# Attention's value products: three single-pass matmuls on split operands against plain float32 in two column halves, with a written order on TensorE

## The chip, the cores and the metric

The kernel runs on one core of one Trainium2 chip. The metric is the device time of one execution in microseconds (us); the number given for a kernel is the median of several runs. TensorE (PE in the profile, PEld for its weight loads) multiplies matrices into PSUM banks, VectorE (DVE), ScalarE (ACT) and GpSimd (POOL) do the element-wise work, SyncE (SP) issues the DMAs.

## What is computed

Two layers over 1024 latent tokens and 256 context tokens of width 1024, all in float32. Each layer normalises and modulates its input, projects it to queries, keys, values and a gate, attends, and projects back. Layer 0 is grouped-query attention (16 heads of 64, 4 key/value heads) for latent and context tokens; layer 1 is latent attention (16 heads, queries and keys of 96, values of 64) for latent tokens alone. Latent queries read all 1280 keys, context queries the 256 context keys. The part that the change touches:

```python
def gqa_attend(q, k, v):
    s = jnp.einsum('bqhgd,bkhd->bhgqk', q, k).astype(jnp.float32) * (GQA_HEAD_DIM ** -0.5)
    p = jax.nn.softmax(s, axis=-1).astype(v.dtype)
    return jnp.einsum('bhgqk,bkhd->bqhgd', p, v)
...
    y = (o * jax.nn.silu(g)) @ p["w_out"]
```

## The kernel before

**Precision.** Most products are made of three matmuls: each operand is split in a high part (rounded to the one-pass type float32r) and a low part (the rest), and high x high, high x low and low x high add up in PSUM (`mm3`, lines 85 to 87; the split, lines 78 and 79). A few small products, such as the modulation ones of line 211, are given to TensorE in plain float32; the profile shows each of those as two matmul instructions, and their operands lie on strips of 32 output partitions, four strips to a bank.

**Stages.** Modulation vectors, keys and values of layer 0, queries, gates, attention of layer 0, its output projection (which also prepares layer 1), then keys and values, queries, gates, attention and output projection of layer 1. What a stage hands to a later one goes through DRAM. Values go there as two arrays, `vdh` and `vdl`, with columns of the constant 2 and 0 beside each head's 64 columns (`v_stages`), so that a value matmul of 128 columns gives a head's outputs and its softmax sums (doubled) at once; the gate is stored doubled as well.

**Attention** (`class Attention`). A unit of work is one head with its 1024 queries and ten key tiles of 128 (`lat`), or, in layer 0, the four heads of a key group with the context queries and two key tiles (`ctx`): 16 + 4 units in layer 0, 16 in layer 1. For each unit:

- Ten *maxima* (`do_max`, lines 364 to 372): two matmuls of 512 columns (or four of 256) fill the scratch tile `mx`, of which there is one, and a DVE reduction takes the maximum of each query row. `do_shift` turns the result with a matmul against the identity (L383) and a DMA puts it as an extra row into the query operand, so that the score matmul subtracts it. Maxima are made ahead: `lead` steps before the scores need them.
- For each key tile, *scores* (`do_scores`): four matmuls in layer 0, six in layer 1, into one of two tiles `st` (L421); two exponentials of it on ACT, `ph` in float32r and `p32` in float32 (L424, L426); their difference `pl` on DVE (L428).
- For each key tile, *values* (`do_av`, L442): six matmuls, three products for each half of 512 queries.
- At its end `finish`: the outputs are copied from PSUM (L465), the sums go by DMA into 128 rows, are inverted on DVE (L489), go to a DRAM row, come back spread over 64 partitions (L494); GpSimd multiplies by the gate and by the outputs (L502, L503), and a DMA stores them. These steps are deferred by one to five key tiles (`later`).

`run` goes through the key tiles: scores, whatever is deferred, a maximum, then the values of the key tile before. The order on TensorE there is chosen by the scheduler that builds the program; elsewhere a block `with in_order(engine)` keeps the written order. The output projection (`out_proj`) starts on the first seven pairs of heads and takes the eighth when the last units are stored.

Of the kernel before, what the change touches and what calls it, by code (L numbers as in the profile page):

```python
# [10 lines left out]
F32 = mybir.dt.float32  # L11
# [8 lines left out]
P = 128  # L20
# [15 lines left out]
def hybrid_kernel(ctx: ExitStack, tc: tile.TileContext, ins: dict, out: bass.AP):  # L36
# [15 lines left out]
    pool.memset(mhalf, -0.5)  # L52

# [14 lines left out]
    vdh = [dram.tile([4, TT, P, w], F32, name=f"vdh{w}") for w in (192, 384)]  # L68
    vdl = [dram.tile([4, TT, P, w], F32, name=f"vdl{w}") for w in (192, 384)]
# [246 lines left out]
    class Attention:  # L316
        def __init__(self, l, units, ops):
# [9 lines left out]
            self.todo = []  # L327

# [7 lines left out]
        def open_late(self, st, stp):  # L336
            l = self.l
            self.op = st.enter_context(tc.tile_pool(name=f"op{l}", bufs=2, reuse_waits="tile"))
            self.vp = stp.enter_context(tc.tile_pool(name=f"vp{l}", bufs=self.ops["vbufs"], reuse_waits="tile"))
            self.pp = stp.enter_context(tc.tile_pool(name=f"pp{l}", bufs=3, reuse_waits="tile"))  # L340
# [4 lines left out]
        def load_v(self, u):  # L345
            key = (u["vg"], u["vc"])
            if key not in self.vcache:
                vs = {}
                for kt in u["kts"]:
                    a = self.vp.tile([P, self.ops["vw"]], F32R, name="vh", tag="vh")  # L350
                    b = self.vp.tile([P, self.ops["vw"]], F32R, name="vl", tag="vl")
                    sp.dma_start(raw(a), vdh[self.l][u["vg"], kt][:, u["vc"]:u["vc"] + 192])
                    sp.dma_start(raw(b), vdl[self.l][u["vg"], kt][:, u["vc"]:u["vc"] + 192])
                    vs[kt] = (a, b)
                self.vcache = {key: vs}
            return self.vcache[key]
# [17 lines left out]
        def do_shift(self, u):  # L374
# [6 lines left out]
            def turn():  # L381
                t = self.ps_m.tile([P, 1024], F32, name="mx", tag="mx")
# [5 lines left out]
            self.later((1, turn))  # L388
# [26 lines left out]
        def do_scores(self, u, kt):  # L415
# [7 lines left out]
            ph = self.pp.tile([P, 1024], F32R, name="ph", tag="ph")  # L423
            act.activation(ph, ps, AF.Exp, scale=self.ops["scale"])  # L424
            p32 = self.pp.tile([P, 1024], F32, name="p32", tag="p32", bufs=2)
            act.activation(p32, ps, AF.Exp, scale=self.ops["scale"])  # L426
            pl = self.pp.tile([P, 1024], F32R, name="pl", tag="pl")
            dve.tensor_sub(pl, p32, raw(ph))  # L428
            return ph, pl

        def do_av(self, u, kt, ph, pl):
            s = self.state[id(u)]
            first, last = kt == u["kts"][0], kt == u["kts"][-1]
            if first:
# [9 lines left out]
            if last:  # L444
                self.finish(u)
# [848 lines left out]
```

## Time and profile before

| | us |
|---|---|
| median of 3 runs | 1961.7 (1961.02 to 1970.17) |
| the profiled execution, device time | 1965.52 |
| its span, first to last instruction | 1963.7 |
| TensorE busy | 1887.5 (96%) |
| VectorE busy | 1321.9 (67%) |
| ScalarE busy | 932.1 (47%) |
| GpSimd busy | 557.1 (28%) |

The granted TensorE clock has a mean of 0.987 of full speed. A matmul's row has the start and a modelled duration that overlaps with the next one's; what a stream of matmuls costs is read from the distance of the starts. "Idle before, releaser" names what ended an engine's idle time.

### The profile page before, as it was taken

The page shows a single profiled execution, that of the slowest core. Times are in us where ns is not written, and L with a number is a line of the kernel's source. Part 1 is how long each engine was busy: PE and PEld are TensorE (multiplying, and loading weights), DVE is VectorE, ACT ScalarE, POOL GpSimd, SP SyncE. Part 2 cuts the span into 40 slices and gives each one's busy share as a digit, 9 for nine tenths or more (in the row PEclk, how much of TensorE's full clock was granted, in tenths as well). Part 3 has the DMA queues.
Part 4 walks back from the last instruction along what each step waited for, and adds up shares of the span by engine and source line. Part 5 has one row for each costly group of instructions (what it writes and reads, how often), then busy time and mean ns, then how long its engine had stood idle before and what let it go on. Part 6 is the DMA issues. An engine that isn't in the chain of part 4 may idle for free. (4 is left out here: it accounts for less than half of the span.)

```text
span 1963.7 us, 24408 instructions
## 1 busy us (share of the span) xinstructions
PE 1887.5 (96%) x8728; PEld 1502.7 (77%) x8728; DVE 1321.9 (67%) x1722; ACT 932.1 (47%) x1254; POOL 557.1 (28%) x438
## 2 busy tenths in 40 slices
PE   7889999999999999998989999999999999999999
PEld 2676668777777777776878788977888888888777
DVE  3764541378898899873566766746777787777632
ACT  2421221066676667772234533325666666666610
POOL 2553431022312222123235544423121212121221
PEclk9999999999999999999999999999999999999999
DMA  7676753342422423115445886675434343433152
GB/s 269 223 248 195 238 166 113 95 141 60 108 77 77 119 58 96 49 37 156 129 128 172 284 250 176 181 210 177 120 98 115 105 122 96 115 103 85 27 177 92
DMA packets 249265, 269.54 MB, mean 137 GB/s; under 512 B 34872, under 2 KB 197416, under 8 KB 249144
## 3 DMA queue, kind: packets, MB, share of 16 engines
q1 hardware_dynamic: 249144, 267.98, 46.4%
q8 instruction: 70, 1.15, 0.2%
q14 instruction: 51, 0.42, 0.1%
HBM read 176.94 MB, written 90.67 MB: 136 GB/s over the span
## 5 line engine op out<-in xcount | busy, mean ns | idle before, releaser
L428 DVE TENSOR_TENSOR pl<-p,ph 128x1024 fp32r<-128x1024 f32 x328 | 442.3, 1349 | 93.8 <-ACT p L426 90.3
L424 ACT ACTIVATE ph<-st 128x1024 fp32r<-128x1024 f32 x328 | 337.3, 1028 | 330.9 <-PE st L421 330.9
L366 DVE TENSOR_REDUCE mA<-mx 128x1 f32<-128x1024 f32 x256 | 312.6, 1221 | 109.8 <-PE mx L364 107.5
L426 ACT ACTIVATE p<-st 128x1024 f32<-128x1024 f32 x328 | 334.7, 1020 | 0.0
L502 POOL TENSOR_TENSOR rb<-rb,sg 64x1024 f32<-64x1024 f32 x32 | 81.7, 2554 | 607.1 <-DMA rb<-rrow 577.0
L442 PE MATMUL av<-pl,vh 128*128 128x512 f32 x656 | 214.7, 401 | 10.9 <-DVE pl L428 10.4
L442 PE MATMUL av<-ph,vh 128*128 128x512 f32 x656 | 216.1, 400 | 1.1 <-ACT ph L424 0.9
L442 PE MATMUL av<-ph,vl 128*128 128x512 f32 x656 | 215.1, 392 | 0.0
L442 PEld LDWEIGHTS av<-pl,vh 128*128 128x128 f32 x656 | 120.1, 188 | 52.3 <-DVE pl L428 28.3
L128 POOL TENSOR_TENSOR wb<-wraw,wa 128x512 fp32r<-128x512 f32 (+3 forms) x69 | 91.7, 1349 | 202.6 <-ACT wa L147 202.5
L442 PEld LDWEIGHTS av<-ph,vl 128*128 128x128 f32 x656 | 123.3, 188 | 28.4
L442 PEld LDWEIGHTS av<-ph,vh 128*128 128x128 f32 x656 | 117.2, 189 | 29.1 <-ACT ph L424 2.1
L85 PE MATMUL mm<-wa,hh 128*128 128x512 f32 (+2 forms) x320 | 122.9, 384 | 5.3 <-ACT hh L285 2.5
L87 PE MATMUL mm<-wa,hl 128*128 128x512 f32 (+2 forms) x320 | 119.2, 374 | 0.5 <-DVE hl L128 0.5
L86 PE MATMUL mm<-wb,hh 128*128 128x512 f32 (+2 forms) x320 | 118.7, 371 | 0.0
L85 PE MATMUL y<-wa,oh 128*128 128x512 f32 x288 | 115.9, 402 | 2.6 <-ACT oh L568 2.5
L87 PE MATMUL y<-wa,ol 128*128 128x512 f32 x288 | 114.7, 400 | 2.2 <-DVE ol L569 2.2
L86 PE MATMUL y<-wb,oh 128*128 128x512 f32 x288 | 114.8, 399 | 0.0
L421 PE MATMUL st<-QA,KA 128*128 128x512 f32 x336 | 107.3, 394 | 0.0
L421 PE MATMUL st<-QB,KB 65*128 65x512 f32 x336 | 106.6, 396 | 0.0
L503 POOL TENSOR_TENSOR os<-os,rb 64x1024 f32<-64x1024 f32 x32 | 102.7, 3208 | 2.5
L372 DVE TENSOR_REDUCE mB<-mx 128x4 f32<-128x1024 f32 x72 | 87.9, 1221 | 21.9 <-PE mx L370 21.8
(211 smaller groups left out, 3625.1 us busy)
## 6 DMA issues: line engine op xcount, KB each, us to landing
mraw<-in_l_w_mod SPq DMA_DIRECT2D x96, 256.0 KB
wraw<-in_l_w_in SPq DMA_DIRECT2D x28, 512.0 KB
vh<-vdh SPq DMA_DIRECT2D x122, 96.0 KB
vl<-vdl SPq DMA_DIRECT2D x122, 96.0 KB
vdh<-vsth SPq DMA_DIRECT2D x30, 384.0 KB
vdl<-vstl SPq DMA_DIRECT2D x30, 384.0 KB
xt<-in_x SPq DMA_DIRECT2D x16, 512.0 KB
wraw<-in_l_w_out SPq DMA_DIRECT2D x16, 512.0 KB
```

The costliest lines, as they stand in the source:

```text
L85: pe.matmul(ps, lhsT=lh(k), rhs=rh(k), start=first and i == 0, stop=False)
L86: pe.matmul(ps, lhsT=lh(k), rhs=rl(k), start=False, stop=False)
L87: pe.matmul(ps, lhsT=ll(k), rhs=rh(k), start=False, stop=last and i == len(ks) - 1)
L128: eng.tensor_sub(lo, a, b)
L366: dve.reduce_max(s["mA"][:, i:i + 1], m, axis=AX.X)
L372: dve.reduce_max(s["mB"][:, 4 * i:4 * i + 4], m.rearrange("p (a b) -> p a b", a=4), axis=AX.X)
L421: pe.matmul(ps[:, n * 512:(n + 1) * 512], lhsT=lh, rhs=rf(n), start=(j == 0), stop=(j == len(prods) - 1))
L424: act.activation(ph, ps, AF.Exp, scale=self.ops["scale"])
L426: act.activation(p32, ps, AF.Exp, scale=self.ops["scale"])
L428: dve.tensor_sub(pl, p32, raw(ph))
L442: pe.matmul(s["av"][n], lhsT=v[:, c0:c0 + P], rhs=src[:, n * 512:(n + 1) * 512], start=first and f, stop=last and e)
L503: pool.tensor_mul(o[sl, :], o[sl, :], rb[sl, :])
```

## The change

- **Value products.** Values are stored once, in float32, without constant columns (`vd`), and loaded as one tile for all heads (layer 0) or for two heads (layer 1). `do_av` multiplies p and v in plain float32: one matmul of 64 columns for the first 512 queries into partitions 0 to 63 of a bank, one for the other 512 into partitions 64 to 127.
- **Exponential.** One, in float32; no difference.
- **Sums.** `add_up` adds the p tiles of a unit: tiles 1, 3 and 5 on DVE (two additions, each in two halves of 512 columns), tiles 0, 2, 4, 6, 7, 8, 9 and the DVE sum on GpSimd (seven additions). The last unit of a layer is shared otherwise. `total_up` then sums over partitions with four matmuls against a tile of twos, on four strips of 32 partitions, in the unit's own PSUM tile, and copies the result on ACT.
- **Order.** `run` goes through pairs of key tiles, with TensorE in written order: a maximum, what is deferred, the values of the last but one pair, a maximum, the scores of this pair. What a unit's end defers comes 4 to 12 key tiles later (`lag`). The turned maxima go into the PSUM tile of the unit that ended last (`spare`), two steps later instead of one. `lead` is 14 instead of 12 and 13.
- **Unit's end.** Outputs lie as 128 x 512, so GpSimd's two products are 128 x 512; four DMAs read the sums, two each move gate, inverse and output.

```diff
         def load_v(self, u):
-            key = (u["vg"], u["vc"])
+
+            key, w = u["vg"], self.ops["vw"]
             if key not in self.vcache:
...
+                v = self.vp.tile([P, TT, w], F32, name="v", tag="v")
+                c0 = key[1]
+                sp.dma_start(v, vd[self.l][key[0]].rearrange("t p n -> p t n")[:, :, c0:c0 + w])
+                self.vcache[key] = v
...
             def turn():
-                t = self.ps_m.tile([P, 1024], F32, name="mx", tag="mx")
+                t = self.spare
+                if t is None:
+                    t = self.ps_m.tile([P, 1024], F32, name="mx", tag="mx")
                 pe.transpose(t[:8, :P], c, ident)
...
-            self.later((1, turn))
+            self.later((2, turn))
...
-            ph = self.pp.tile([P, 1024], F32R, name="ph", tag="ph")
-            act.activation(ph, ps, AF.Exp, scale=self.ops["scale"])
-            p32 = self.pp.tile([P, 1024], F32, name="p32", tag="p32", bufs=2)
-            act.activation(p32, ps, AF.Exp, scale=self.ops["scale"])
-            pl = self.pp.tile([P, 1024], F32R, name="pl", tag="pl")
-            dve.tensor_sub(pl, p32, raw(ph))
-            return ph, pl
-
-        def do_av(self, u, kt, ph, pl):
+            p = self.pp.tile([P, 1024], F32, name="p", tag="p")
+            act.activation(p, ps, AF.Exp, scale=self.ops["scale"])
+            self.add_up(u, kt, p)
+            return p
+
+        def add_up(self, u, kt, p):
...
+            by_dve = i % 2 == 1 or i > 5 if tail else i in (1, 3, 5)
+
+            def add(who, p):
+                if who not in sums:
+                    sums[who] = (p, False)
+                    return
+                a, own = sums[who]
+                t = a if own else self.ap.tile([P, 1024], F32, name="ac" + who, tag="ac" + who)
+                if who == "p":
+                    pool.tensor_add(t, a, p)
+                else:
+                    for n in range(2):
+                        ns = slice(n * 512, n * 512 + 512)
+                        dve.tensor_add(t[:, ns], a[:, ns], p[:, ns])
+                sums[who] = (t, True)
+
+            add("d" if by_dve else "p", p)
+            if last:
+                a, b = ("d", "p") if tail or len(u["kts"]) == 2 else ("p", "d")
+                add(a, sums[b][0])
+                s["total"] = sums[a][0]
+
+        def do_av(self, u, group):
...
+            for kt, p in group:
+                for n in range(2):
+                    pe.matmul(s["av"][64 * n:64 * n + 64, :], lhsT=s["v"][:, kt, u["vc"]:u["vc"] + 64],
+                              rhs=p[:, n * 512:(n + 1) * 512], start=kt == kts[0], stop=kt == kts[-1])
...
+            def total_up():
+                t = s["av"]
+                for q in range(4):
+                    pe.matmul(t[32 * q:32 * q + 32, :256], lhsT=twos, rhs=s["total"][:, q * 256:q * 256 + 256],
+                              start=True, stop=True)
+                act.copy(rb[:, :256], t[:, :256])
+                for q in range(4):
+                    sp.dma_start(cs[32 * q:32 * q + 32, :], rb[32 * q:32 * q + 1, :256])
...
-            self.later((1, invert), (2, spread), (3, scale), (5, store))
...
+            self.later((self.lag, total_up), (self.lag + 2, invert), (self.lag + 4, spread), (self.lag + 6, scale),
+                       (self.lag + 8, store))
+
+        lag = 4
...
+            pairs = [(t, u, u["kts"][i:i + 2]) for t, u in enumerate(self.units) for i in range(0, len(u["kts"]), 2)]
+            with in_order(mybir.EngineType.PE):
+                for t, u, kts in pairs:
...
+                    self.maxima(self.step - base + 1 + lead, t + 1 + ahead)
                     self.run_deferred(self.step)
...
+                    if len(held) == 2:
+                        self.do_av(*held.pop(0))
+                    self.maxima(self.step - base + 2 + lead, t + 1 + ahead)
+                    held.append((u, [(kt, self.do_scores(u, kt)) for kt in kts]))
```

TensorE in layer 0's loop before, one key tile and the start of the next (names are output, then moving and stationary operand, each with its buffer's number):

```order
L421 MATMUL st_4002<-QA_3635,KA_2948 128x512 x2
L421 MATMUL st_4002<-QB_3636,KB_2949 128x512 x2
L364 MATMUL mx_4014<-KA_2948,QA_3905 128x512 x2
L442 MATMUL av_3994<-ph_3981,vh_3407 128x512
L442 MATMUL av_3995<-ph_3981,vh_3407 128x512
L442 MATMUL av_3994<-ph_3981,vl_3408 128x512
L442 MATMUL av_3995<-ph_3981,vl_3408 128x512
L442 MATMUL av_3994<-pl_3985,vh_3407 128x512
L442 MATMUL av_3995<-pl_3985,vh_3407 128x512
L421 MATMUL st_4024<-QA_3635,KA_2948 128x512 x2
```

The same place in the loop of the change, one pair of key tiles (lines from 50 on have moved: L423 is the score matmul, L471 the value matmul):

```order
L364 MATMUL mx_4066<-KA_3976,QA_3982 128x512 x2
L471 MATMUL av_4072<-p_4016,v_3402 64x512 x2
L471 MATMUL av_4072<-p_4023,v_3402 64x512 x2
L364 MATMUL mx_4077<-KA_3976,QA_3982 128x512 x2
L423 MATMUL st_4081<-QA_3689,KA_2934 128x512 x2
L423 MATMUL st_4081<-QB_3690,KB_2935 128x512 x2
L423 MATMUL st_4089<-QA_3689,KA_2934 128x512 x2
L423 MATMUL st_4089<-QB_3690,KB_2935 128x512 x2
```

Twelve value matmuls for two key tiles have become four, and they stand between two maxima, with the scores behind them. Once a unit, its end stands there as well; TensorE in layer 0's loop of the change, at the pair where a unit's total (L515) and the turned maxima (L385) are due:

```order
L370 MATMUL mx_3903<-KA_2934,QA_3894 128x256 x4
L515 MATMUL av_3653<-acp_3629,twos_76 32x256 x4
L385 MATMUL av_3653<-ident_69,mC_3875 8x128
L471 MATMUL av_3864<-p_3842,v_3402 64x512 x2
L471 MATMUL av_3864<-p_3851,v_3402 64x512 x2
L370 MATMUL mx_3926<-KA_2934,QA_3894 128x256 x4
```

L385 writes into av_3653, the bank that L515 has just filled and that ACT copies in between; both stand ahead of the values. In the program of the change this is so in 12 pairs of layer 0 and 14 of layer 1. VectorE in the loop of the change, from a unit's last maxima on (L366 and L372 reduce maxima, L453 adds p, L387 makes the extra query row, L523 inverts sums):

```order
L372 TENSOR_REDUCE mB_3495<-mx_3647 128x4
L453 TENSOR_TENSOR acd_3638<-p_3594,p_3636 128x512 x2
L372 TENSOR_REDUCE mB_3495<-mx_3658 128x4
L379 TENSOR_TENSOR mC_3664<-mA_3494,mB_3495 128x8
L366 TENSOR_REDUCE mA_3694<-mx_3696 128x1
L453 TENSOR_TENSOR acd_3638<-acd_3638,p_3679 128x512 x2
L387 TENSOR_SCALAR crow_3710<-av_3459 8x128
L366 TENSOR_REDUCE mA_3694<-mx_3717 128x1
L523 RECIPROCAL cr_3747<-cs_3617 128x8
```

Before, a subtraction (L428) followed each reduction; now a unit's two additions stand between the two reductions of its third and its fourth pair.

178 lines of the change are left out of this document (64 added, 114 removed).

## Prediction

> **What bounds the kernel now.** I read the busy times first, then the two attention stages as windows, then one key tile in the timeline. Part 1 of the page:
>
> ```profile
> PE 1887.5 (96%) x8728; PEld 1502.7 (77%) x8728; DVE 1321.9 (67%) x1722; ACT 932.1 (47%) x1254; POOL 557.1 (28%) x438
> ```
>
> TensorE (PE) is the only engine near full; GpSimd (POOL) has most room. The windows view of the two stages, each from its first score matmul to its last value matmul (columns: length, then busy time and count of PE, weight loads, DVE, ACT, POOL, then clock, DMA share, GB/s):
>
> ```profile
> 403.10:889.80 486.70, 477.31 (x2086) 371.18 (x2085) 423.13 (x376) 344.99 (x380) 110.83 (x45) 1.00 0.30 82
> 1349.50:1868.60 519.10, 516.49 (x2281) 419.04 (x2281) 396.90 (x363) 320.70 (x341) 110.53 (x50) 1.00 0.38 104
> ```
>
> Together 1005.8 us, over half of the span, at full clock; the change works here. One key tile of layer 0, PE's timeline (start, duration, instruction):
>
> ```profile
> 614.07 0.63 PE L421 MATMUL st<-QA,KA 128*128 128x512 f32 x2
> 614.53 0.62 PE L364 MATMUL mx<-KA,QA 128*128 128x512 f32 x2
> 615.00 0.64 PE L421 MATMUL st<-QB,KB 65*128 65x512 f32 x2
> 615.47 0.63 PE L442 MATMUL av<-ph,vh 128*128 128x512 f32 x2
> ...
> 616.40 0.62 PE L442 MATMUL av<-pl,vh 128*128 128x512 f32 x2
> 616.87 0.62 PE L421 MATMUL st<-QA,KA 128*128 128x512 f32 x2
> ```
>
> Durations overlap, so starts count: from 614.07 to 616.87 twelve matmuls issue in 2.80 us, 0.233 us each, without a gap. Four are scores, two a maximum, six the values. So PE's matmul count sets these stages. Groups of the page, and the longest wait of PE's weight loads there:
>
> ```profile
> L442 PE MATMUL av<-ph,vh 128*128 128x512 f32 x656 | 216.1, 400 | 1.1 <-ACT ph L424 0.9
> ```
> ```profile
> PEld av L442 <- DVE pl L428: 28.3, 46, 1.6
> ```
>
> 656/2 = 328 key tiles, 168 in layer 0 and 160 in layer 1. At 0.233 us a matmul, layer 0 would take 168 x 10 x 0.233 + 156 maxima x 0.467 = 465 us, and 487 are measured: 22 us are waits, mostly for the split of p (L428). Layer 1 (six score matmuls, about 146 maxima in the loop): 160 x 12 x 0.233 + 68 = 516 of 519 us.
>
> **The change part by part.**
>
> *Value products.* Six single-pass matmuls a key tile go (1.40 us); two plain float32 matmuls of 64 columns come, on separate column halves. The trace has no 64-column one, but the modulation matmuls (L211) are plain float32, 32 columns wide, on four column strips. One alone (two passes), then four on four strips, between single-pass neighbours:
>
> ```profile
> 29.39 0.40 PE L85 MATMUL mm<-wa,hh 128*128 128x512 f32 x1
> 29.72 1.04 PE L211 MATMUL pm<-mraw,s 128*32 128x512 f32 x2
> 30.70 0.50 PE L85 MATMUL mm<-wa,hh 128*128 128x512 f32 x1
> 31.03 0.62 PE L86 MATMUL mm<-wb,hh 128*128 128x512 f32 x2
> ```
> ```profile
> 261.40 0.39 PE L87 MATMUL mm<-wa,hlc 128*128 128x512 f32 x1
> 261.72 1.06 PE L211 MATMUL pm<-mraw,s 128*32 128x512 f32 x8
> 262.72 0.50 PE L85 MATMUL mm<-wa,hhc 128*128 128x512 f32 x1
> 263.05 0.39 PE L86 MATMUL mm<-wb,hhc 128*128 128x512 f32 x1
> ```
>
> From neighbour to second neighbour 1.64 us and 1.65 us; less the two neighbours' own 0.47 that is 1.17 and 1.18. Four strips cost what one costs: they run side by side. For two rounds on the same strips, the weight loads:
>
> ```profile
> 48.10 0.16 PEld L211 LDWEIGHTS pm<-mraw,s 128*32 128x32 f32 x8 [0.36 <-DMA w_k<-in_l_k_norm]
> ...
> 48.99 0.12 PEld L211 LDWEIGHTS pm<-mraw,s 128*32 128x32 f32 x2 [0.31 <-issue]
> ```
>
> The second pass pair starts 0.89 us after the first, so a round more costs 0.87 or so, and the new step, two key tiles at a time, 1.18 + 0.87 = 2.05 us against 2.80. Of 164 pairs each saves 0.75: **-123 us** (84 pairs in layer 0: -63; 80 in layer 1: -60). The ends for the second half of the columns: free, as these rows say, or behind the first with two passes more, 0.86 us a key tile. I take free, four strips being a harder case than two.
>
> Each strip needs two weight loads a round, and the row at 48.10 has all eight begun and ended within 0.16 us, though one takes 0.11 us by itself (a load of 128 columns 0.19):
>
> ```profile
> L211 PEld LDWEIGHTS pm<-mraw,s x192: 106/109/155, 4.3 to 269.0; 128*32 128x32 f32 x192
> ```
> ```profile
> L442 PEld LDWEIGHTS av<-pl,vh 128*128 128x128 f32 x656 | 120.1, 188 | 52.3 <-DVE pl L428 28.3
> ```
>
> So they lie beside each other and beside matmuls, and cost the sum nothing. [...]
>
> *Maxima, in written order.* The scratch bank mx has one buffer, so a maximum waits for the DVE reduction before it:
>
> ```profile
> 621.56 1.22 DVE L366 TENSOR_REDUCE mA<-mx 128x1 f32<-128x1024 f32 x1
> ...
> 622.90 0.67 PE L364 MATMUL mx<-KA,QA 128*128 128x512 f32 x2
> ```
> ```profile
> 1381.84 0.63 PE L364 MATMUL mx<-KH,QH 96*128 96x512 f32 x2
> ...
> 1382.51 1.22 DVE L366 TENSOR_REDUCE mA<-mx 128x1 f32<-128x1024 f32 x1 [0.52 <-PE mx L364]
> ```
>
> 0.67 to the reduction, 1.22 in it, 0.12 back: 2.0 us from one maximum to the next. In a pair they stand 0.47 + 2.05 = 2.5 us apart over the values and 0.47 + 1.87 = 2.3 us over the scores (layer 1: 3.3), so they just fit, as long as DVE does nothing else. Where two stand together, PE idles 2.0 - 0.47 = 1.53; the written order has twelve such places in layer 0, after context heads and at the start: **+18**.
>
> *Row sums.* They leave the value matmul and become additions. DVE adds p in two halves of 512 after each of two of a unit's ten key tiles, between the two reductions; GpSimd does seven additions of 128x1024 and two products of 128x512. Nearest rows:
>
> ```profile
> L502 POOL TENSOR_TENSOR rb<-rb,sg x32: 2387/2467/3080, 443.0 to 1879.7; 64x1024 f32<-64x1024 f32 x32
> ```
> ```profile
> L585 DVE TENSOR_TENSOR xt<-xt,yt x18: 680/692/1704, 906.7 to 1959.9; 128x512 f32<-128x512 f32 x18
> ```
> ```profile
> L720 POOL TENSOR_TENSOR t<-t,t 128x512 f32<-128x512 f32 x16 | 20.5, 1283 | 0.0
> ```
>
> GpSimd: 7 x 2.47 + 2 x 1.28 = 19.9 us a unit of 25 to 31 us, so it keeps up. DVE: 4 x 0.69 = 2.8, while ten subtractions of 1.23 go. But the two engines block each other:
>
> ```profile
> 597.82 3.27 POOL L503 TENSOR_TENSOR os<-os,rb 64x1024 f32<-64x1024 f32 x1
> ```
> ```profile
> 599.89 2.29 DVE L428 TENSOR_TENSOR pl<-p,ph 128x1024 fp32r<-128x1024 f32 x1
> ...
> 603.23 1.21 DVE L428 TENSOR_TENSOR pl<-p,ph 128x1024 fp32r<-128x1024 f32 x1
> ```
>
> GpSimd ends at 601.09 and the DVE operation 1.09 later: it stood still meanwhile. In the third pair of a unit GpSimd starts its first addition at about 0.3 us (exponential of the third key tile done) and ends at 2.8; DVE's first half, due at 1.9, ends at 3.4, the second at 4.1, the second reduction at 5.4, against the next maximum in layer 0 at 4.85 (two maxima 0.93, values 2.05, eight score matmuls 1.87): 0.6 us late, and more when GpSimd still holds work of the unit before. I take 1.5 a unit, ends 0 and 5: **+24** in layer 0; layer 1's pair is 5.78 us long and hides it. What is queued behind the late half on DVE is the reduction, and for that PE waits.
>
> *The total.* Four 32-column matmuls of 256 columns (about half of the 1.18), a copy of 128x256 on ACT, and then, in 26 of the pairs, the transpose L385 into the same bank, which must wait for that copy:
>
> ```profile
> L704 ACT ACTIVATE sq<-mm 128x256 f32<-128x256 f32 x10 | 3.8, 380 | 15.3 <-PE mm L87 14.2 <-POOL hl L128 1.1
> ```
>
> With 0.7 for the matmuls, 0.1, 0.38 and 0.1 for the hand-overs, and 0.3 for the transpose: 1.6 us; alone 0.6. 26 x 1.6 + 10 x 0.6 = 47.6: **+25** in layer 0, **+24** in layer 1 (rounded up for transposes alone). ACT's second exponential goes, which nobody waits for then.
>
> *V and DMAs.* 244 loads of vh and vl become 9 of v. The first in layer 0 has 1.31 MB. In layer 1's projection stage the DMAs moved 260 GB/s (last column):
>
> ```profile
> 1045.00:1170.00 125.00, 119.81 (x657) 105.54 (x655) 84.89 (x179) 58.99 (x137) 62.20 (x71) 0.99 0.83 260
> ```
>
> At that rate the load takes 5 us, and two pairs, 9.7 us, stand ahead of the first value matmul; I put 2 us a layer (ends 0 and 5) for its late start: **+4**. SP loses 235 of these issues and gains about as many (four reads of the sums instead of one, two rows instead of one for sg, rb and od), so its queue is no fuller.
>
> *Projection stages.* The split of V goes. PE waits for it in layer 1's stage:
>
> ```profile
> PE mm L85 <- DVE vstl L79: 2.0, 1, 2.0
> PE mmk L85 <- DVE vstl L79: 1.5, 2, 1.1
> ```
>
> Those and a little in layer 0: **-5**, ends 0 and -15.
>
> *Ends of the stages.* The last heads' sums pass through reciprocal, row and broadcast:
>
> ```profile
> 900.44 0.40 PE L87 MATMUL y<-wa,ol 128*128 128x512 f32 x1
> 902.81 0.73 PE L85 MATMUL y<-wa,oh 128*128 128x512 f32 x1 [1.97 <-ACT oh L568]
> ```
>
> Already now PE waits there in layer 0. A unit's output is now stored six pairs after its last values instead of five key tiles, so more of this chain lies behind the loop: **+4**, ends 0 and 10. In layer 1, three row tiles of output products, 126 x 0.233 = 29 us, cover it.
>
> **Sum.** Layer 0: 465 - 63 + 18 + 24 + 25 + 2 = 471, against 487: -16. Layer 1: 516 - 60 + 24 + 2 = 482, against 519: -37. With +4 and -5: **-54 us**. The profiled execution took 1965.5 us (span 1963.7 and 1.8 around it) and so becomes 1911.5; the median shown, 1961.7, is 3.8 lower: **1908 us**.
>
> **Rivals.**
>
> *Queues (1948 us).* DVE and GpSimd meet at each half, so that both halves wait for a whole addition. This needs GpSimd behind by one operation at the third pair, for which the busy 19.9 of 25 us speak, and the product L531, which waits for a DMA ahead of an addition; the room of 5 us speaks against it. Price: 3.5 us more a unit in layer 0 and 1.5 in layer 1 at the full, 80 us; half of it gives 1948, all of it 1988.
>
> *The halves run one behind the other (2190 us, slower).* Each key tile then costs 0.86 more, 328 x 0.86 = 282. The decisive point: the gain of 54 us is gone as soon as the second half adds 54/328 = 0.165 us. Against it stand the rows at 29.72 and 261.72.
>
> [...]
>
> *Fewer waits (1875 us).* No blocking in layer 0 (-24) and nearly the full -15 in the projections (-9 more).
>
> **Chances and range.** Forecast, 1885 to 1935: 0.55. Fewer waits, below 1885: 0.11. Queues, 1935 to 1990: 0.22. Halves in turn 0.08, loads 0.04. A measurement tells about 0.5% here, 10 us: faster takes the first two and half of the queues, 0.77; same 0.06; slower 0.17. The range 1868 to 1975 leaves out the last two (0.12), the worse end of the queues (0.05) and little below (0.02).
>
> **What would show it.** In the trace after, the two halves of a value matmul should start within hundredths of a microsecond, and a pair of key tiles take 2.05 us of values between maxima. PE's waits for mA, mB and the transposes should total about 70 us, those for p none. If first starts of the halves stand 0.8 us apart, the forecast is wrong; if DVE's additions last over 2 us each, the queues have it; a new chain with GpSimd in it at the total would break the step on its room.

## The result and the profile after

The changed kernel took 1942.9 us (median of four runs, 1934.7 to 1946.0); the kernel before, beside it on the same chip, 1963.3 us. The ratio is 0.988, 95% interval 0.984 to 0.992: faster by 20 us, where 54 were forecast. The time lies inside the stated range, but the gain is far short of the forecast. The profiled execution is the fastest of the four, 1934.7 us, 31 us below the profiled one of before. The forecast had 1911.5 us for it, so the profile shows 23 of the 35 us by which the median misses 1908; the rest is spread between executions.

Where the 31 us are can be read from the two attention stages, from the first score matmul to the last value matmul. The windows view of the changed kernel (columns as in the prediction, granted clock third from the end):

```profile
402.10:901.10 499.00, 445.38 (x1890) 234.33 (x1888) 274.36 (x277) 183.80 (x208) 317.34 (x154) 0.93 0.25 65
1357.00:1837.30 480.30, 470.71 (x2081) 278.06 (x2081) 244.22 (x262) 181.12 (x196) 313.80 (x157) 0.99 0.36 88
```

Layer 1 went from 519 to 480 us, 39 less; forecast were 37. Layer 0 went from 487 to 499, 12 more; forecast were 16 less. What lies between the stages went from 460 to 456 us, the start and the end of the span together are within 1 us of before. So the whole miss of the profiled execution sits in layer 0. There TensorE is busy for 445 of 499 us, where it was busy for 477 of 487 before, and its clock is 0.93 instead of 1.00.

The new value products are not the reason. PE's timeline in the changed kernel, one steady pair of layer 0:

```profile
530.79 0.63 PE L364 MATMUL mx<-KA,QA 128*128 128x512 f32 x2
531.35 1.94 PE L471 MATMUL av<-p,v 128*64 128x512 f32 x8
533.22 0.72 PE L364 MATMUL mx<-KA,QA 128*128 128x512 f32 x2
...
535.65 0.63 PE L364 MATMUL mx<-KA,QA 128*128 128x512 f32 x2
```

Two halves of two key tiles with two passes each are eight instructions in 1.94 us; the step from the maximum before to the maximum behind it (530.79 to 533.22) is 2.43 us, of which 0.47 are the maximum's own, so 1.96 are left for the values. The whole pair, from 530.79 to 535.65, takes 4.86 us; the prediction built 4.85 from its parts.

The same view some microseconds earlier shows the loss. A unit's first maximum waits, two more follow in a row, and then everything is slow:

```profile
513.27 0.63 PE L423 MATMUL st<-QB,KB 65*128 65x512 f32 x2
518.37 0.94 PE L364 MATMUL mx<-KA,QA 128*128 128x512 f32 x2 [4.46 <-DMA QA<-q0h]
520.62 1.22 PE L364 MATMUL mx<-KA,QA 128*128 128x512 f32 x2 [1.31 <-DVE mA L366]
523.15 1.22 PE L364 MATMUL mx<-KA,QA 128*128 128x512 f32 x2 [1.31 <-DVE mA L366]
524.30 3.68 PE L471 MATMUL av<-p,v 128*64 128x512 f32 x8
```

The value step that takes 1.94 us at 531 takes 3.68 at 524. The clock column of three windows tells why (before the wait's end, behind it, and after):

```profile
511.00:518.00 7.00, 2.90 (x12) 1.43 (x8) 0.00 (x0) 1.95 (x2) 6.77 (x4) 1.00 0.55 130
518.00:528.90 10.90, 7.90 (x16) 2.90 (x17) 3.67 (x3) 0.00 (x0) 6.66 (x4) 0.53 0.25 61
528.90:540.00 11.10, 11.10 (x47) 6.47 (x46) 7.25 (x7) 5.24 (x7) 1.16 (x1) 1.00 0.68 159
```

For 10.9 us the chip granted TensorE about half of its clock (0.53). Then it is back at 1.00. The same stands behind the wait of 4.5 us that ends at 482.2: 0.55 for 10.2 us. That idle TensorE brings the drop on, in the wait of 4.46 us and in the pauses of 1.31 us behind it, was the author's theory, which these windows alone do not show (idle_filled_all below bears on this).

What the waiting matmuls wait for is in the waits view of layer 0, PE alone (us in total, times, longest):

```profile
PE mx L364 <- DVE mA L366: 11.8, 9, 1.3
PE mx L364 <- DMA QA<-q0h: 8.9, 2, 4.5
PE mx L364 <- issue: 8.8, 2, 4.5
PE av L385 <- ACT rb L517: 5.9, 12, 0.5
PE av L515 <- ACT os L493: 5.6, 1, 5.6
PE mx L364 <- DVE mB L372: 5.0, 3, 2.4
PE mx L370 <- DMA QA<-q0h: 4.5, 2, 3.1
```

In the kernel before, the same view of layer 0 has four rows, none for queries:

```profile
PE av L442 <- DVE pl L428: 7.9, 18, 1.0
PE mx L364 <- DVE mA L366: 1.3, 1, 1.3
PE av L442 <- ACT ph L424: 0.9, 2, 0.4
PE av L442 <- ACT osc L465: 0.2, 1, 0.2
```

The transfer that the first maxima wait for is issued by SP only when the scores just before have run. SP's timeline at the place above, and what SP's queue waited for in layer 0:

```profile
513.46 1.11 SPq L837 DMA_DIRECT2D QA<-q0h  x2
```
```profile
SPq L837 <- PE st L423: 33.0, 11, 6.9
```

So the chain is this. A query tile has three buffers. Near a context unit, which lasts one pair, the lead of 14 key tiles would reach into a fourth unit; the limit bars that until the next unit begins. Then three things fall on one spot of the written order: the fourth unit's queries are sent for into the buffer that the last score matmul has just released (513.46), the maximum that needs them starts 4.9 us later, and the barred maxima must be caught up one behind another. The values are written behind that maximum, and TensorE starts nothing ahead of it: the 4.46 us of idle time in the timeline above.

### The profile page after: what moved, and what is told of

Same layout as the page of the kernel before. It is cut to its first block, busy times and chain, and to the rows that moved or that the text cites. A ratio compares the mean times of both kernels' runs of the same rounds, so it can differ in the third digit from the quotient of the medians.

```text
span 1932.8 us, 23525 instructions
## 1 busy us (share of the span) xinstructions
PE 1806.6 (93%) x8360; PEld 1225.4 (63%) x8360; DVE 1003.9 (52%) x1494; ACT 633.1 (33%) x942; POOL 959.9 (50%) x648
## 5 line engine op out<-in xcount | busy, mean ns | idle before, releaser
L366 DVE TENSOR_REDUCE mA<-mx 128x1 f32<-128x1024 f32 x256 | 313.3, 1224 | 378.2 <-PE mx L364 377.9
L449 POOL TENSOR_TENSOR acp<-acp,p 128x1024 f32<-128x1024 f32 x156 | 370.2, 2373 | 238.0 <-ACT p L426 232.5
L471 PE MATMUL av<-p,v 128*64 128x512 f32 x1312 | 330.7, 625 | 1.0 <-ACT rb L517 1.0
L471 PEld LDWEIGHTS av<-p,v 128*64 128x64 f32 x1312 | 82.1, 140 | 149.6 <-issue 139.8
L364 PE MATMUL mx<-KA,QA 128*128 128x512 f32 x256 | 95.8, 458 | 40.2 <-DVE mA L366 14.5
L372 DVE TENSOR_REDUCE mB<-mx 128x4 f32<-128x1024 f32 x72 | 87.8, 1219 | 68.1 <-PE mx L370 67.8
L449 POOL TENSOR_TENSOR acp<-p 128x1024 f32<-128x1024 f32 x32 | 76.5, 2391 | 74.5 <-ACT p L426 73.8
L364 PEld LDWEIGHTS mx<-KA,QA 128*128 128x128 f32 x256 | 45.1, 203 | 103.2 <-DVE mA L366 52.4
L423 PE MATMUL st<-QA,KA 128*128 128x512 f32 x336 | 107.8, 402 | 0.0
L423 PE MATMUL st<-QB,KB 65*128 65x512 f32 x336 | 106.5, 398 | 0.0
L423 PE MATMUL st<-QH,KH 97*128 97x512 f32 x320 | 102.2, 400 | 1.3 <-DMA QH<-crow 1.3
L423 PE MATMUL st<-QL,KH 96*128 96x512 f32 x320 | 102.2, 400 | 0.6 <-DVE gth L311 0.6
L86 PE MATMUL mm<-hh,wa 128*128 128x512 f32 x256 | 102.2, 399 | 0.2 <-DVE qt L1182 0.2
L88 PE MATMUL mm<-hh,wb 128*128 128x512 f32 x256 | 101.8, 398 | 0.0
```

Of the source, the lines that this page charges most:

```text
L86: pe.matmul(ps, lhsT=lh(k), rhs=rh(k), start=first and i == 0, stop=False)
L88: pe.matmul(ps, lhsT=ll(k), rhs=rh(k), start=False, stop=last and i == len(ks) - 1)
L364: pe.matmul(m[:, n * 512:(n + 1) * 512], lhsT=s["mq"][:, i * P:(i + 1) * P], rhs=s["mk"][:, n * 512:(n + 1) * 512], start=True, stop=True)
L366: dve.reduce_max(s["mA"][:, i:i + 1], m, axis=AX.X)
L372: dve.reduce_max(s["mB"][:, 4 * i:4 * i + 4], m.rearrange("p (a b) -> p a b", a=4), axis=AX.X)
L423: pe.matmul(ps[:, n * 512:(n + 1) * 512], lhsT=lh, rhs=rf(n), start=(j == 0), stop=(j == len(prods) - 1))
```

## The experiments

Times are medians; ratios are to the kernel before, run beside each, with 95% interval. "Layer 0", "layer 1" and "between" are the stretches above, in each run's profiled execution; a stage differs between executions by some us (halves_apart, which costs what the change costs, has layer 0 at 503 where the change has 499).

**Queries in a buffer of their own (own_q).** Layer 0's first three context units get a query buffer of their own, so that three remain for the others.

```diff
-        QA = qp.tile([P, NL], F32R, name="QA", tag="QA")
-        QB = qp.tile([65, NL], F32R, name="QB", tag="QB")
+        own = at.qc if not lat and g != 2 else qp
+        QA = own.tile([P, NL], F32R, name="QA", tag="QA")
+        QB = own.tile([65, NL], F32R, name="QB", tag="QB")
```

> The query tiles of the first three context heads get a buffer of their own; the written order and its limit of units stay. Theory A (in layer 0 TensorE stands four times 4.45 us and once 3.1 us before the first maximum of a new unit, because that unit's queries are loaded into a buffer that the scores just before it set free, and the clock then runs at half for some 10 us): these waits get shorter or go, layer 0's 499 us fall by 20 to 45 us, the time from 1943 to about 1905. The three maxima in a row stay, since the limit stays. Theory B (additions on VectorE and GpSimd hold up layer 0): nothing changes, 1935 to 1950. Theory C (only the order limit matters, the load is issued when the maxima are, whatever buffer is free): the waits stay at 3 to 4.5 us, 1935 to 1950.

Measured: 1907.9 us, ratio 0.971 (0.968 to 0.974), 35 us less than the change. Layer 0:

```profile
402.70:869.70 467.00, 434.22 (x1890) 231.03 (x1888) 273.38 (x277) 183.96 (x208) 317.76 (x154) 0.97 0.28 69
```

32 us less, with layer 1 unchanged at 480.0 and the clock back to 0.97. No wait of PE for queries is left in layer 0; the waits of 1.3 us between maxima stay (11.8 us in 9). So A holds, and C falls: the issue does come earlier once the buffer is free. 22 of the 32 us are the waits themselves (8.9 + 8.8 + 4.5; two of them had no releaser in the profile, but they went with the rest). The other 10 are put down to the slow matmuls behind them; idle_filled_all below tests that.

**And the limit one unit further (own_q_ahead3).**

```diff
-    at.run(14, 2, pieces)
+    at.run(14, 3, pieces)
```

> As own_q, and in layer 0 a unit may begin its maxima three units ahead instead of two. Theory A: waits for queries and maxima in a row both go; layer 0 comes to 499 - 21 (waits) - 12 (maxima in a row) - 20 to 26 (half clock) = 440 to 450 us, the time to 1885 to 1895. Theory B (additions): at most the 12 us of maxima in a row, about 1930. Theory C: as A, and own_q does not.

Measured: 1892.3 us, ratio 0.963 (0.960 to 0.966), the time that A expected. Layer 0 is at 459.0, 8 us less than in own_q, and 9 to 19 short of what A expected for it. Two waits ahead of the first maximum of a unit have come in the place of the maxima in a row. One is 4.6 us, for VectorE, whose additions take 6.6 us there beside GpSimd. The other is 3.8 us, and not for VectorE, as the expectation of all_four has it, but for queries once more:

```profile
PE mx L365 <- DMA QA<-q0h: 3.8, 1, 3.8
```

This load was not held by its buffer. It left SP's queue at 670.14 us, right behind the store of an output that had waited 7.8 us for GpSimd's product, and the maximum started at 674.91.

**Is the low clock a cost of its own (idle_filled, idle_filled_all)?** The changed kernel works through its waits. First only through the wait for queries:

```diff
                     self.start_unit()
+                    if self.barred:
+                        self.barred = False
+                        m = self.ps_m.tile([P, 1024], F32, name="mx", tag="mx")
+                        for _ in range(18):
+                            pe.matmul(m[:, 0:512], lhsT=k[:, 0:P], rhs=k[:, 0:512], start=True, stop=True)
```

> The changed kernel with 18 needless matmuls of 0.233 us (4.2 us) ahead of the first maximum of each unit of layer 0 that the limit held back; their results are overwritten. The wait for the queries stays as long, but TensorE works in it. Theory A1 (the half clock after each idle stretch is a cost of its own): the granted clock in layer 0 goes from 0.93 towards 1.00 and the time falls by 10 to 25 us, to about 1920 to 1930. Theory A2 (the low clock comes from something else, such as the new mix of matmuls): clock and time stay, or the time grows by up to 10 us.

Measured: 1937.5 us, ratio 0.985 (0.981 to 0.989); layer 0 at 496.0, clock 0.95. Too little to decide: the pauses between the maxima in a row were still there, and the clock fell behind them (0.83 and 0.89 for 10 us at two of three places, 1.00 at the third). So five more went into each such pause:

```diff
+                if self.catch:
+                    self.catch -= 1
+                    if self.catch < 2 and self.spare is not None:
+                        for _ in range(5):
+                            pe.matmul(self.spare, lhsT=self.k[:, 0:P], rhs=self.k[:, 0:512], start=True, stop=True)
```

> idle_filled with five more needless matmuls (1.17 us) in each of the pauses of 1.32 us between the maxima in a row that follow a wait for queries. TensorE then works through both, and the maxima come no earlier. Theory A1 (TensorE's low clock in layer 0 is caused by the idle stretches, and costs of itself): the granted clock in layer 0 goes from 0.93 to 0.98 or more, and the matmuls behind the waits take 1.95 us for a pair of values instead of 3.4; layer 0 falls by 8 to 15 us, to 484 to 491. Theory A2 (something else lowers it): clock at 0.93 to 0.95 and layer 0 at 495 or more.

Measured: 1929.6 us, ratio 0.980 (0.978 to 0.982). Layer 0, and PE's timeline at one of its waits:

```profile
406.80:896.00 489.20, 464.73 (x2025) 256.71 (x2023) 274.51 (x277) 184.04 (x208) 317.81 (x153) 0.97 0.26 66
```
```profile
485.43 4.26 PE L420 MATMUL mx<-KA 128*128 128x512 f32 x18
490.04 0.70 PE L366 MATMUL mx<-KA,QA 128*128 128x512 f32 x2 [0.35 <-DMA QA<-q0h]
490.58 1.29 PE L425 MATMUL av<-KA 128*128 128x512 f32 x5
492.06 0.74 PE L366 MATMUL mx<-KA,QA 128*128 128x512 f32 x2 [0.18 <-DVE mA L368]
492.64 1.32 PE L425 MATMUL av<-KA 128*128 128x512 f32 x5
494.12 0.74 PE L366 MATMUL mx<-KA,QA 128*128 128x512 f32 x2 [0.15 <-DVE mA L368]
494.78 1.94 PE L486 MATMUL av<-p,v 128*64 128x512 f32 x8
```

The first maximum starts no earlier behind its scores than without the filling, yet the values behind it take 1.94 us again, and needless work made the kernel some 13 us faster (10 of them in layer 0). A1 holds; the clock itself, 0.97, missed the expected 0.98 by a little. Around two of the filled waits, from 482 to 500 us and from 518 to 536, it is 1.00; where in the layer it still falls was not shown.

**The additions left out (no_sums).**

```diff
-            add("d" if by_dve else "p", p)
+            sums["p"] = sums["d"] = (p, False)
```

> Leaves out the additions of p on VectorE and GpSimd: the total is taken of one key tile's p, with 1 added before the reciprocal, so the output is not the reference's. Theory A: additions cost TensorE two waits of 2.4 us in layer 0 and nothing in layer 1: 1930 to 1943. Theory B (my forecast's 24 us in layer 0, and more if the queues hold each other up): 1905 to 1920.

Measured: 1909.8 us, ratio 0.972 (0.970 to 0.975). Layer 0 takes 476.1 us, 23 less, layer 1 476.6, 4 less. Theory B had the better number. Two things are gone. One is the waits of 2.4 us for VectorE, one of which reads like this in the changed kernel (whole timeline):

```profile
569.14 4.43 DVE L453 TENSOR_TENSOR acd<-p 128x512 f32<-128x512 f32 x2
...
570.19 2.82 POOL L449 TENSOR_TENSOR acp<-p 128x1024 f32<-128x1024 f32 x1
...
573.10 2.69 POOL L449 TENSOR_TENSOR acp<-acp,p 128x1024 f32<-128x1024 f32 x1
573.49 1.21 DVE L372 TENSOR_REDUCE mB<-mx 128x4 f32<-128x1024 f32 x1
...
574.76 0.73 PE L364 MATMUL mx<-KA,QA 128*128 128x512 f32 x2 [2.39 <-DVE mB L372]
```

VectorE's two halves of 0.68 us each take 4.43 beside GpSimd, the reduction comes late, the next maximum waits; this is the prediction's "queues" in small, with slow matmuls behind it again (a value step of 3.57 us starts at 576.77, and the clock is 0.50 from 576.70 to 580.10). So a wait of 2.4 us, too, was followed by the half clock. The other is the end of the layer: the wait of 5.6 us for an output buffer (L515 behind L493 in the waits above) is gone with GpSimd's queue. Of the 23 us, 15.5 are won by the last wait for queries (853 us in the changed kernel) and 7 behind it; of the 15.5, the two waits with what is slow behind them are about 10 (4.3 and 5.5 us, by the starts of the scores in both traces), the rest is spread over the layer in small steps. The waits for queries are still there (four of 4.3 to 4.5 us, one of 3.3), so this is a second cause and not the same one.

**Without the written order (no_order).** TensorE's order in the attention stages is the scheduler's again.

```diff
-            with in_order(mybir.EngineType.PE):
+            with ExitStack():
```

> The changed kernel with the value products as they are, and TensorE's order in the attention stages left to the scheduler, as before the change. Theory A (layer 0 loses by the written order: a matmul that is not ready stands ahead of others that are): the waits for queries are covered by scores and values as in the kernel before, layer 0 comes to 430 to 460 us and the time to 1875 to 1905; layer 1 stays within 10 us of 480. Rival E (the written order is what lets the new products be as cheap as they are, by keeping two passes of the same kind together): each change between kinds of matmul costs some 0.2 us more, and the time is 1950 or above.

Measured: 1960.0 us, ratio 0.996 (0.994 to 0.999), nearly nothing gained on the kernel before and 17 us more than the change. Layer 0 takes 518.9 us although TensorE hardly waits (507 busy, clock 1.00):

```profile
400.20:919.10 518.90, 507.16 (x1890) 236.26 (x1890) 285.57 (x278) 188.11 (x211) 321.85 (x155) 1.00 0.25 63
```

Theory A expected 430 to 460, so this part of it fell: order costs waits, but it also gives something. PE's timeline in this kernel:

```profile
600.40 1.07 PE L471 MATMUL av<-p,v 128*64 128x512 f32 x2
601.41 0.73 PE L364 MATMUL mx<-KA,QA 128*128 128x512 f32 x2
602.07 1.93 PE L471 MATMUL av<-p,v 128*64 128x512 f32 x6
```

One half of one key tile (its two passes) runs alone in 1.07 us, and the six instructions left take 1.93, as long as eight do. A round is one instruction, or two on the two halves that start together. Counting starts in layer 0's trace: the changed kernel has its 672 value instructions in 84 stretches and 336 rounds of two; this one has 158 stretches and 480 rounds, 288 of them with one half alone. At the 0.43 us of a round, the 144 more are 62 us; TensorE's busy time grew by as much (445 to 507 us). Rival E had the time right (above 1950), but the rounds, which it did not count, outweigh the changes between kinds of matmul, which it did (148 more, 30 us at the 0.2 us of its estimate).

**Do halves have to be neighbours (halves_apart)?** The written order stays, but a pair issues both key tiles for the first 512 queries and then both for the second.

```diff
-            for kt, p in group:
-                for n in range(2):
+            for n in range(2):
+                for kt, p in group:
```

> The changed kernel with the value matmuls of a pair issued half by half: both key tiles for the first 512 queries, then both for the second. If the two halves run beside each other only when they stand next to each other in the order, seven rounds of 0.47 us take the place of four: 1.4 us a pair, 164 pairs, 230 us more, about 2170, and so no_order (which pulls halves apart) loses by this. If TensorE finds the other half anyway: within 10 us of 1943, and no_order's loss has another cause.

Measured: 1941.8 us, ratio 0.987 (0.986 to 0.988), as the change itself. PE's timeline, one pair:

```profile
535.51 0.63 PE L364 MATMUL mx<-KA,QA 128*128 128x512 f32 x2
536.07 1.94 PE L471 MATMUL av<-p,v 128*64 128x512 f32 x8
537.94 0.72 PE L364 MATMUL mx<-KA,QA 128*128 128x512 f32 x2
```

My first theory here failed by 230 us. The two halves still start together, 0.013 us apart instead of 0.007, although all four instructions of the first half are written ahead of those of the second. The author reads this as TensorE starting a matmul of the second half ahead of one of the first half that is written before it. (The trace does not number the instructions; that the written order reached TensorE is taken from the kernel, and the doubled distance fits it.) It was seen within a stretch of value matmuls. What no_order pays for, by its 480 rounds against 336, is other matmuls between the halves.

**Total and transpose in different pairs (turn_later, own_q_turn, total_earlier).** In the changed kernel the transpose waits for ACT's copy out of the bank that both use (whole timeline, one of 26 places):

```profile
547.09 0.64 PE L515 MATMUL av<-acd,twos 128*32 128x256 f32 x8
...
547.80 0.37 ACT L517 COPY rb<-av 128x256 f32<-128x256 f32 x1
...
548.22 0.27 PE L385 MATMUL av<-ident,mC 128*8 128x128 f32 x1 [0.49 <-ACT rb L517]
...
548.42 0.65 PE L471 MATMUL av<-p,v 128*64 128x512 f32 x2
```

From 547.09 to 548.42 the place takes 1.33 us. First the transposes went one pair later:

```diff
-            self.later((2, turn))
+            self.later((4, turn))
```

> The transposed maxima one pair later than the total, so that the transpose does not wait for the copy of the sums out of the same bank. My forecast priced total and transpose together at 1.6 us and the total alone at 0.6: of 26 places each saves 0.6 to 0.8, so 15 to 20 us less, 1923 to 1930. Rival (the transpose waits for the copy of another unit, or the row of maxima comes late for the scores): 1940 to 1960.

Measured: 1931.8 us, ratio 0.983 (0.982 to 0.985): 11 us less than the change, 4 in each layer by the profiled executions, and so a little short of the 15 to 20 expected. Layer 1 gave part back at its start, where the first unit's row now comes late:

```profile
1368.67 1.19 PE L423 MATMUL st<-QH,KH 97*128 97x512 f32 x2 [5.29 <-DMA QH<-crow]
```

On top of own_q_ahead3:

> own_q_ahead3 with the later transposes, without the third output buffers. From own_q_ahead3's parts: layer 0 459 - 4, layer 1 478 - 4, the stretch between them 454, 96 and 400 around them: about 1884. If the end of layer 0 takes back what the layer gains, as in all_four: 1888 to 1892.

Measured: 1884.6 us, ratio 0.959 (0.957 to 0.961); layer 0 448.8, layer 1 476.7, between them 458.6. The time that the sum of the parts gave.

The other way round, the total and all behind it one pair earlier, and the transposes as they were:

```diff
-        lag = 4
+        lag = 2
```

> own_q_ahead3 with the total, and all that follows it, one pair of key tiles earlier, so that total and transpose lie in different pairs. If the copy between them is what they cost (as turn_later says, 4 us in each layer) and GpSimd has the sums ready by then: layers 0 and 1 fall by 4 us each, and the end of layer 0 by up to 5: 1880 to 1885. If GpSimd does not have the sums ready: TensorE waits in written order for them, up to 36 times some 2 us, 1900 to 1960.

Measured: 1871.6 us, ratio 0.952 (0.950 to 0.954), the fastest kernel of the study together with best_of_parts below, 71 us below the change and 93 below the kernel before beside it, and 8 below the better end of what was expected. Both stages, granted almost the full clock:

```profile
403.80:846.50 442.70, 425.96 (x1890) 231.67 (x1888) 278.74 (x277) 184.01 (x208) 317.39 (x153) 0.98 0.29 73
1302.40:1771.20 468.80, 466.04 (x2079) 275.97 (x2081) 246.51 (x263) 181.31 (x196) 315.27 (x158) 1.00 0.37 91
```

Layer 1 is 9 us below own_q_ahead3, whose waits for the copy are 7.5 us there; layer 0 is 16 below. No wait for the copy is left (own_q_ahead3 has 5.9 us in layer 0), but that is not all: the 3.8 us wait for queries and the 4.6 us one for VectorE are gone or short as well, and the wait of 5.7 us at the end of the loop now stands behind the stage. What setting total and transpose apart gained by itself was not separated from that. GpSimd has the sums ready but for four times in layer 0 (PE's waits there), and never late in layer 1:

```profile
PE av L516 <- POOL acp L450: 6.2, 4, 2.0
```

**The end of layer 0 (out_buffers3, all_four, tail_on_vector, all_five, best_of_parts).** At the end the changed kernel waits 5.6 us in the loop, ahead of a total, and behind the loop 6.1 us ahead of another total and 3.3 us in the output products. First a third buffer for a unit's output:

```diff
-            self.op = st.enter_context(tc.tile_pool(name=f"op{l}", bufs=2, reuse_waits="tile"))
+            self.op = st.enter_context(tc.tile_pool(name=f"op{l}", bufs=3 - l, reuse_waits="tile"))
```

> Three buffers instead of two for a unit's output, reciprocal row and gate in layer 0. Theory A (at the end of layer 0 the copy of the values waits for the store of an earlier unit, 14.7 and 6.4 us, and TensorE behind it 5.6 us and once more 6.1 us in the output products): the end of the stage is 6 to 12 us shorter, 1931 to 1937. Rival (GpSimd's backlog of additions delays the same chain whatever the buffers): within 3 us of 1943.

Measured: 1943.3 us, ratio 0.990 (0.988 to 0.992), no gain. Layer 0 is 4 us shorter, which is no more than executions differ, and the stretch between the layers 11 longer: the output products now wait for the last unit's stores. PE's share of the waits there:

```profile
PE y L86 <- ACT oh L594: 15.9, 3, 10.1
```

All parts so far but the earlier total together:

> Own query buffers, three units ahead, three output buffers and the later transposes together. If their gains add up: 1892 - 8 (end of layer 0) - 17 (transposes) = 1867. If the waits for VectorE that own_q_ahead3 showed (4.6 and 3.8 us ahead of maxima) grow when TensorE runs closer to its room: 1880 or above.

Measured: 1888.4 us, ratio 0.961 (0.959 to 0.963). Layer 0 takes 441.7 us, and the stretch between the layers 468.8 instead of own_q_ahead3's 453.8: the gain at the end of the loop is given back whole. Then the additions of layer 0's last three units went to VectorE:

```diff
-            tail = u is self.units[-1]
+            tail = u in self.units[-1 if self.l else -3:]
```

> own_q_ahead3 with the additions of layer 0's last three units (not of the last alone) given mostly to VectorE, which has no maxima left to reduce there. Theory F (GpSimd's queue of additions delays the products, stores and buffers at the end of layer 0: its product stands 10 us behind additions after its data was sent for, and TensorE waits 5.7, 6.0 and 3.4 us): the stretch from layer 0's last value matmul to layer 1's first scores and the wait of 5.7 us before it shrink by 8 to 15 us together, the time from 1892 to 1877 to 1884. Rival G (the chain of small transfers sets the end, whoever adds): within 4 us of 1892.

> all_four with the additions of layer 0's last three units on VectorE. Theory F: the 15 us that all_four lost between the layers (468.8 against 453.8) come back in good part, 1872 to 1880. Rival G: 1886 to 1890.

> total_earlier with three output buffers and the additions of layer 0's last three units on VectorE. In all_five these two took 4 us off own_q_turn. Theory F (GpSimd's backlog and the output buffers hold the end of layer 0): total_earlier's 2.0 us ahead of the total and some 9 us in the output products go in part, 1863 to 1869. Rival G (the chain of transfers sets that end): 1870 to 1874.

Measured: tail_on_vector 1890.3 us (0.9625, 0.960 to 0.965), the same as own_q_ahead3 within the interval: the wait of 5.7 us in the loop is down to 0.8, the stretch behind it 6 us longer. all_five 1880.9 us (0.957, 0.956 to 0.959), 8 less than all_four and 4 less than own_q_turn, between what F and G expected. best_of_parts 1871.5 us (0.952, 0.950 to 0.953), the same as total_earlier. So GpSimd's queue and the buffers hold some waits there, but taking them away moves the wait along: from total_earlier on, the end of layer 0 seems to be set by the chain that nobody shortened (sums, reciprocal, row, broadcast, product, store, load). Two of the three times are G's; that the chain sets the end was not shown by shortening it, and which of its links is the longest was not tried.

## Why the prediction was wrong, point by point

**Value products: right.** 2.05 us a pair were forecast and 1.96 came between the maxima; a steady pair as a whole takes 4.86 against a built 4.85, so a pair saves 0.74 us where 0.75 were forecast. The halves start 0.007 us apart. Layer 1, which has little else in the way, fell by 39 us against 37.

**Maxima, in written order: the step that failed.** It counted twelve places of 1.53 us in layer 0, +18, and looked only at the reduction as what a maximum waits for. The places cost less (11.8 us in nine waits), but five of the maxima stood first in a unit, and a first maximum also needs its queries. In the kernel before no wait of PE for queries appears in layer 0, and in no_order, where the scheduler orders the same matmuls, TensorE is idle for 11.7 of 518.9 us, whatever it waits for; once the order is written, the load is in the path: 22 us of waits. And the sum took the clock of before, 1.00, for granted: the waits made it 0.93, some 10 us more behind the waits for queries alone (own_q by difference, idle_filled_all by filling them). 32 us, shown by own_q taking them out. With this step mended the forecast's time came, 1907.9 us against 1908 and layer 0 at 467 against 471, though not every term of it was right, as the next ones show.

**Additions on VectorE and GpSimd: near in size, in another place.** Forecast were 24 us in layer 0 and none in layer 1; without them layer 0 is 23 us shorter and layer 1 is 4. But they do not cost 1.5 us in each unit. They cost two waits of 2.4 us with slow matmuls behind them (about 10 us), some 5 us in small steps, and about 7 us at the end of the layer, where GpSimd's queue holds the output buffers. That the sum of these came out at the forecast's 24 is luck.

**Total and transpose: right in size.** 1.6 us a place forecast, 1.33 measured. That it was a cost to be avoided, and not only to be counted, turn_later shows (11 us).

**V and DMAs, projections, ends.** No wait for v shows in either stage. Everything outside the two stages was forecast at +4 - 5 = -1 us and came to about -4. The ends of layer 0 were put at +4; TensorE's waits there are 5.6 us in the loop and 6.1 + 3.3 behind it.

**The sum for layer 0.** 471 were forecast and 499 came. The waits for queries (22) and the clock behind them (10) add 32; the smaller maxima in a row take off 6, the totals with a transpose (12 of 1.33 instead of 1.6) 3, v 2 and the additions 1. That gives 491; the other 8 us were not taken apart.

**The signs.** The prediction said that PE's waits for mA, mB and the transposes should total about 70 us. They are 24 us in layer 0 (11.8 + 5.0 + 5.9 + 1.3) and 8 in layer 1: part of what the additions cost stands under other names, the 5.6 us for an output buffer and the slow matmuls. Of the other signs, the halves start together and no wait of PE for p is in the views.

**The rivals.** The halves did not run one behind the other (they start 0.007 us apart), nor did the weight loads, to which the forecast gave a chance of 0.04, stand in the way: eight loads and eight matmuls of a value step fit in 1.94 us. The loads of the step at 531.35:

```profile
531.35 0.20 PEld L471 LDWEIGHTS av<-p,v 128*64 128x64 f32 x4 [0.37 <-issue]
531.83 0.14 PEld L471 LDWEIGHTS av<-p,v 128*64 128x64 f32 x2 [0.29 <-issue]
532.26 0.14 PEld L471 LDWEIGHTS av<-p,v 128*64 128x64 f32 x2 [0.28 <-issue]
```

The queues' rival named a mechanism that is there at two places, and a time, 1948 us, that is close to the measured one for another reason. None of the rivals had the transfer of the queries in it.

## What to carry to other kernels

Before an order is written by hand, list for each instruction everything it waits for, transfers and the buffers they go to included: a wait that a scheduler covered without anybody seeing it can become a stall in the written order. Then look where the written order bunches such instructions (here the one-pair units), and give those a buffer more or an earlier start. And do not count a stall of TensorE at its length alone: here 22 us of waits cost 32, for the matmuls behind them ran slower (a value step of 3.68 us instead of 1.94).

## What the runs showed of the hardware

- A wait of 4.5 us, with two pauses of 1.3 us behind it, was followed by 10.9 us at a granted clock of 0.53. Filling only the wait left 0.83 and 0.89 for 10 us at two places; filling the pauses too brought the value step behind them from 3.68 back to 1.94 us. Needless matmuls made the kernel faster (1942.9 to 1929.6 us). Two waits of 2.4 us were followed by slow matmuls too: a clock of 0.50 from 576.70 to 580.10 us and from 712.00 to 716.50, with value steps of 3.57 and 3.68 us.
- With the two column halves apart in the written order (halves_apart), a value step stays at 1.94 us and the halves start 0.013 us apart, where the change has 0.007; the times are 1941.8 and 1942.9 us. With other matmuls between them (no_order), one half of one key tile took 1.07 us alone and the six instructions left 1.93.
- Beside GpSimd's additions VectorE's of 128x512, 0.68 us alone, took up to 2.9 us:

```profile
L453 DVE TENSOR_TENSOR acd<-p x40: 675/1507/2879, 411.7 to 892.7; 128x512 f32<-128x512 f32 x40
```
